# Up projection of a streaming encoder step: the loads of the sample weights are ordered behind the raw weights of the next feature tile

## The chip, the cores and the metric

The kernel runs on one core of one Trainium2 chip. The metric is the device time of one execution in microseconds (us), the median of several runs. One further execution was recorded by the hardware profiler; all durations, starts and waits below are from that recording.

## What is computed

One inference step of a one-layer hybrid encoder, for a prompt of 1024 frames (no history) and a sample of 32 frames (with history), both with 1024 features. A mixer with three kinds of heads comes first, then a convolutional feed-forward block. The change lies in that block:

```python
def conv_ffn(xn, buf, w_up, conv_w, conv_b, w_down):
    up = xn @ w_up                                       # (T, 1024) @ (1024, 5632)
    up, buf = causal_dwconv(up, buf, conv_w, conv_b)     # width 3 along the frames
    gate, val = jnp.split(up, 2, axis=-1)
    return (jax.nn.gelu(gate, approximate=True) * val) @ w_down, buf
...
x = x + rms_norm(h, g_mix_post[l])
h, ffn_buf = conv_ffn(rms_norm(x, g_ffn_pre[l]), states[6][l], ffn_w_up[l], ...)
x = x + rms_norm(h, g_ffn_post[l])
```

Everything is float32. The 5632 columns of `w_up` are 44 tiles of 128 features; tile `f` of the gate half and tile 22+`f` of the value half are worked on together, so there are 22 feature tiles.

## The kernel before

The stages run one behind the other on TensorE: input projection with the mixers beside it, output projection, up projection, down projection. Float32 products are made of three matmuls each (`mm3`): weights' high part by the input's high part (line 88), weights' high by the input's low (line 89), weights' low by the input's high (line 90). So every operand is first split into a high part, by a cast on ScalarE (line 93), and a low part, by a subtraction on VectorE (line 94). The first two matmuls of a weight need its cast alone, the third needs the subtraction too.

**The prompt's up projection** (`up_all`, line 1513) multiplies two by two blocks with a Strassen-like scheme: seven products p1 to p7 instead of eight, each of twelve 128x512 matmuls (four blocks of the inner dimension, three matmuls each), 84 for one feature tile. For feature tile f:

- `up_raw` (line 1278) loads the raw weights: two tiles of 512 KB, `wu{f}r` and `wu{22+f}r`, from `w_up`, on SyncE's queue (line 1282). The pool has two buffers for them, so the loads for tile f+1 wait until VectorE has read the last of tile f's.
- `up_operands` (line 1294) makes the seven weight operands: A12, A11, A22 are the raw blocks, S1 to S4 are sums of them (lines 1306 to 1312, VectorE). Each is split by lines 93 and 94. In the trace they read `A_{f}h` and `S_{f}h`.
- `up_block` (line 1334) issues the products: puy gets A12, pux A11 and then S2 and S3, puw S1 and then S4, puz A22. ScalarE copies some sums out of PSUM (`keep`, line 1347, tiles `c_...`), VectorE adds them into the two tiles `uu` (line 1352).
- `up_finish` (line 1433) convolves the finished `uu` of tile f-1: one activation (line 1440) and two scalar_tensor_tensor (line 1442) for each half, a gelu (line 1444), a product (line 1445), and the store of the result `y` to `h_d` (line 1446, SyncE's queue).

**The sample's up projection** is laid beside it by `up_samples` (line 1448). It is 24 rounds (three column groups, eight blocks of the inner dimension each). A round is a load of sample weights `wus` (line 1457, 1 MB, in the third group 768 KB, SyncE's queue) and three or four small matmuls `us` (line 1474). The loads go into a ring of three buffers; the load for round i+3 is issued in the program after the matmuls of round i and waits for them on the chip. Two or three rounds are visited in each feature tile from f=2 to f=10, between the product S1 or A22 and the product S2, and all later products are ordered behind them by

```python
with tc.issue_after(kept["us"].ins) if "us" in kept else ExitStack():
```

**What sets the order.** The order of the instructions on each engine is made when the kernel is built, by a list scheduler with its own estimate of times. `issue_after(x)` gives it a constraint: what is issued inside isn't placed ahead of `x`. `behind["SP"]` is the latest instruction on SyncE that others are ordered by; `up_raw` sets it to the second raw load (line 1282). The sums of down weights (`sum_weights`, line 1572, DRAM to DRAM, `ws_d`) are already ordered by it. The loads of `wus` had no such constraint. SyncE issues in order: an instruction that waits holds all that are behind it.

Of the kernel before, what the change touches and what calls it, by code (L numbers as in the profile page):

```python
# [78 lines left out]
def body(ctx: ExitStack, tc: tile.TileContext, a: dict):  # L79
    nc = tc.nc  # L80
    act, dve, pool, pe, sp = nc.scalar, nc.vector, nc.gpsimd, nc.tensor, nc.sync
# [157 lines left out]
    cols_of, dcs_of, behind = {}, {}, {}  # L239
    HSET = (2, 0, 4, 5)  # L240
    VGD = (lambda b, h: True, lambda b, h: True, lambda b, h: True)
    pws, wo_raw, ring = ExitStack(), [], []
# [1076 lines left out]
    def behind_products():  # L1319
        with ExitStack() as order:  # L1320
            for x in ends[-3:]:
                order.enter_context(tc.issue_after(x))
            return order.pop_all()
# [124 lines left out]
    def up_samples():  # L1448

        closing = ExitStack()  # L1450
        own = closing.enter_context(tc.tile_pool(name="pss", bufs=1, side="right", reuse_waits="tile"))

        def load(i):
            if i < len(ROUNDS):
                g, k = ROUNDS[i]
                nq = UGROUPS[g][1]
                sp.dma_start(ring[i % 3][:, :nq], a["w_us"][8 * g + k, :, :nq])

        smp_u = own.tile([128, NU, 2 + DEC], F32, name="smp_u")
        sp.dma_start(smp_u[:, :, 0:2], a["fcache"])  # L1460
        ring = [wus[:, 0], wus[:, 1], own.tile([128, 4, 512], F32, name="wus2")]
        smp_x = own.tile([128, 8, DEC], F32, name="smp_x")
        sp.dma_start(smp_x, xn_d[:, :, SEQ:])
        i = 0
        for i in range(3):
            load(i)
        yield
        i = 0
        for g, (c0, nq) in enumerate(UGROUPS):
            ps = psf.tile([128, 512], F32, tag="sx", name=f"us{g}", bufs=1)  # L1470
            for k in range(8):
                with behind_products():
                    for q in range(nq):
                        kept["us"] = pe.matmul(ps[DEC * q:DEC * q + DEC], smp_x[:, k, :], ring[i % 3][:, q, :],
                                               start=k == 0, stop=k == 7)
                load(i + 3)
                i += 1
                if k in VISITS:
                    yield
            m = DEC * nq  # L1480
            us = own.tile([128, NF, DEC], F32, tag="us", name=f"usr{g}", bufs=1).rearrange("p f t -> p (f t)")[:, :512]
            act.copy(us[:m], ps[:m])
            yield
            tp = psb.tile([128, 4, 128], F32, tag="big", name=f"ust{g}", bufs=3)
            for b in range(4):
                pe.transpose(tp[:, b, :m], us[:m, 128 * b:128 * b + 128], ident[:m, :m])
            for b in range(4):
                act.copy(smp_u[:, 4 * c0 + b:4 * (c0 + nq):4, 2:2 + DEC], tp[:, b, :m].rearrange("p (q t) -> p q t", t=DEC))
        pool.tensor_copy(fcq, smp_u[:, :, DEC:DEC + 2])
        yield  # L1490
        smp_y = [p3.tile([128, NF, DEC], F32, tag="xg0", name="smp_v", bufs=1), own.tile([128, NF, DEC], F32, tag="us", name="smp_w", bufs=1)]
        def conv(*args, **kw):
            with tc.issue_after(kept["gated"].ins):
                dve.tensor_tensor(*args, **kw)

        for lo, dst in ((0, smp_h), (NF, smp_y[0])):
            js = slice(lo, lo + NF)
            w = [fconv[:, js, s:s + 1].broadcast_to([128, NF, DEC]) for s in range(4)]
            yield
            conv(dst, smp_u[:, js, 2:2 + DEC], w[2], op=ALU.mult)  # L1500
            yield
            conv(dst, dst, w[3], op=ALU.add)
            for s in range(2):
                yield
                conv(smp_y[1], smp_u[:, js, s:s + DEC], w[s], op=ALU.mult)
                yield
                conv(dst, dst, smp_y[1], op=ALU.add)
        yield
        act.activation(smp_h, smp_h, AF.Gelu_apprx_tanh)
        conv(smp_h, smp_h, smp_y[0], op=ALU.mult)  # L1510
        closing.close()
# [672 lines left out]
```

## Time and profile before

| | us |
|---|---|
| median of 3 runs | 1349.72 |
| the runs | 1347.81, 1349.72, 1349.77 |
| the profiled execution | 1349.57 |
| its span, from the first to the last instruction | 1347.8 |
| output projection of the last tokens ends, up projection begins | at 659 |
| first visit of sample rounds | at 714.6 |
| last sample matmul | at 897.2 |
| last store of `h_d` issued | at 1129.7 |

Times such as "at 714.6" are us from the start of the span. A row of the timeline gives the start, the duration, the engine, the line, the operation with its tiles, the count, and in brackets the idle time of the engine ahead of it with the instruction that ended it. A row of the chain gives the start, the time spent and what; it is the chain of work that ended last, followed back from the end. A row of the windows view gives for a stretch of time the busy time of each engine (the number of instructions), then the granted TensorE clock, the busy share of the DMA engines, and GB/s. TensorE matmuls overlap: a 128x512 one is shown with 0.39 us while the next starts 0.23 us after it.

### The profile page before, as it was taken

Reading aid. Unit: us, or ns where it says so; the run is one execution under the profiler, and the core shown is the slowest. Engines: PE = TensorE matmul, PEld = TensorE weight load, DVE = VectorE, ACT = ScalarE, POOL = GpSimd, SP = SyncE. Lnnn points to the kernel's source line nnn. Section 1 sums busy time; section 2 is a strip of 40 time slices with the busy share of each in tenths; the row PEclk is TensorE's granted clock in tenths of the full one; section 3 lists DMA queues with packets and bytes.
Section 4 is the critical chain, followed back from the end, with each engine's and each line's share of the span. In section 5 each row is a group of like instructions: output and inputs, shape, how many; then the busy total and the mean of one; then the engine's idle time right before and its main releaser. Section 6 shows DMA issues by size and latency. Waiting matters only on the chain.

```text
span 1347.8 us, 25583 instructions
## 1 busy us (share of the span) xinstructions
PE 1302.1 (97%) x9896; PEld 1100.3 (82%) x9896; DVE 1006.8 (75%) x1761; ACT 699.9 (52%) x1298; POOL 281.8 (21%) x400
## 2 busy tenths in 40 slices
PE   6999999999999998999999999999999999999997
PEld 6999889998888987867886767778888887778885
DVE  5795649778698778875797677768888876499566
ACT  5555556554575555534764444445454544454552
POOL 4532303135022254313110010111110000020004
PEclk9999989999998999989999999999999999999999
DMA  9799868886789954543436978865655249844425
GB/s 343 245 354 370 276 230 257 280 281 217 275 246 313 335 190 131 188 134 117 165 106 195 336 212 290 214 191 145 168 153 147 81 137 350 330 161 139 144 88 125
DMA packets 134784, 291.73 MB, mean 216 GB/s; under 512 B 29015, under 2 KB 63991, under 8 KB 132535
## 3 DMA queue, kind: packets, MB, share of 16 engines
q1 hardware_dynamic: 120887, 266.51, 57.8%
q0 software_dynamic: 9264, 19.14, 7.8%
q10 hardware_dynamic: 4512, 4.46, 1.0%
q8 instruction: 77, 1.26, 0.4%
q14 instruction: 44, 0.36, 0.1%
HBM read 229.38 MB, written 85.78 MB: 234 GB/s over the span
## 4 chain that ended last, share of the span: by engine, by line
PE 60%; DVE 8%; ACT 3%; DMA 3%; issue 2%; POOL 1%; SPq 0%; DVEq 0%; POOLq 0%; ACTq 0%
PE pux_None L88 4%; PE pux_None L90 4%; PE pux_None L89 4%; PE q L88 3%; PE q L90 3%; PE q L89 3%; PE puw_None L90 3%; PE puw_None L89 3%; PE puw_None L88 3%; PE x L88 2%; PE x L89 2%; PE x L90 2%; PE zp L90 2%; PE zp L88 2%; PE zp L89 2%
## 5 line engine op out<-in xcount | busy, mean ns | idle before, releaser
L1442 DVE SCALAR_TENSOR_TENSOR y<-uu,fconv_sb,y 128x1024 f32<-128x1024 f32 x88 | 112.7, 1281 | 26.3 <-ACT y L1440 25.4
L1439 POOL COPY fhalo<-uu 128x2 f32<-128x2 f32 x44 | 17.7, 403 | 389.9 <-DVE uu L1352 385.5
L1440 ACT ACTIVATE y<-uu,fconv_sb 128x1024 f32<-128x1024 f32 x44 | 54.7, 1244 | 22.5 <-DVE uu L1352 21.8
L90 PE MATMUL zp<-woh,cl 128*128 128x512 f32 (+1 forms) x144 | 58.2, 404 | 1.5 <-DVE cl L1091 1.5
L88 PE MATMUL zp<-woh,ch 128*128 128x512 f32 (+1 forms) x144 | 57.9, 411 | 1.0 <-ACT ch L1090 0.7
L89 PE MATMUL zp<-wol,ch 128*128 128x512 f32 (+1 forms) x144 | 58.4, 406 | 0.3 <-DVE wol L94 0.3
L88 PE MATMUL pv<-wt_0h,xh 128*128 128x256 f32 (+1 forms) x192 | 55.7, 290 | 3.1 <-DVE xl L319 1.6
L90 PE MATMUL pv<-wt_1h,xl 128*128 128x256 f32 (+1 forms) x192 | 55.1, 287 | 0.0
L88 PE MATMUL pv<-wt_1h,xh 128*128 128x256 f32 (+1 forms) x192 | 54.6, 284 | 0.0
L90 PE MATMUL pv<-wt_0h,xl 128*128 128x256 f32 (+1 forms) x192 | 54.5, 284 | 0.0
L89 PE MATMUL pv<-wt_0l,xh 128*128 128x256 f32 (+1 forms) x192 | 54.3, 283 | 0.0
L89 PE MATMUL pv<-wt_1l,xh 128*128 128x256 f32 (+1 forms) x192 | 54.3, 283 | 0.0
L206 POOL TENSOR_SCALAR hrs<-hss 128x5 f32<-128x5 f32 (+3 forms) x27 | 10.1, 375 | 181.6 <-DVE hss L1000 177.1
L1717 POOL TENSOR_TENSOR gss<-gss 128x1 f32<-128x1 f32 (+1 forms) x9 | 9.9, 1096 | 176.8 <-ACT gjk L1710 176.8
L816 DVE COPY_PREDICATED P<-masks_sb,sc 128x352 f32<-128x352 int32 (+3 forms) x53 | 37.8, 713 | 4.9 <-PE sc L729 4.3
L88 PEld LDWEIGHTS pv<-wt_0h,xh 128*128 128x128 f32 x192 | 35.9, 187 | 4.8 <-DVE xl L319 2.1
L1000 DVE TENSOR_REDUCE hss<-sq 128x5 f32<-128x320 f32 (+3 forms) x27 | 13.5, 502 | 31.5 <-ACT sq L999 31.4
L207 POOL TENSOR_TENSOR hrs<-hrs,mhalf 128x5 f32<-128x5 f32 (+3 forms) x27 | 36.2, 1341 | 2.2
L88 PEld LDWEIGHTS pv<-wt_1h,xh 128*128 128x128 f32 x192 | 36.0, 188 | 0.7 <-issue 0.6
L90 PEld LDWEIGHTS pv<-wt_1h,xl 128*128 128x128 f32 x192 | 36.0, 187 | 0.3
L90 PEld LDWEIGHTS pv<-wt_0h,xl 128*128 128x128 f32 x192 | 36.0, 187 | 0.2
L89 PEld LDWEIGHTS pv<-wt_0l,xh 128*128 128x128 f32 x192 | 36.0, 188 | 0.1
(1899 smaller groups left out, 4645.8 us busy)
## 6 DMA issues: line engine op xcount, KB each, us to landing
wus<-in_w_us SPq DMA_DIRECT2D x16, 1024.0 KB, 6.2
wrP<-in_w_dn SPq DMA_DIRECT2D x27, 512.0 KB, 4.2
ht<-h_d SPq DMA_DIRECT2D x22, 512.0 KB, 7.5
wt_0r<-in_w_tok SPq DMA_DIRECT2D x21, 512.0 KB, 6.0
wt_1r<-in_w_tok SPq DMA_DIRECT2D x21, 512.0 KB, 6.6
h_d<-y SPq DMA_DIRECT2D x21, 512.0 KB, 3.1
ws_d<-in_w_dn POOLq DMA_DIRECT2D x20, 512.0 KB, 6.8
wrP<-ws_d SPq DMA_DIRECT2D x20, 512.0 KB, 3.9
```

The lines of the kernel that those rows point to most:

```text
L88: pe.matmul(ps, lh[0], rh[0], start=first, stop=False, **kw)
L89: pe.matmul(ps, lh[0], rh[1], start=False, stop=False, **kw)
L90: return pe.matmul(ps, lh[1], rh[0], start=False, stop=last, **kw)
L206: pool.tensor_scalar(out, ss, 1.0 / width, eps, op0=ALU.mult, op1=ALU.add)
L207: pool.tensor_tensor(out, out, mhalf[:n, :cols], op=ALU.pow)
L816: dve.copy_predicated(dst, mk.broadcast_to([n, 11, *mk.shape[2:]]), src)
L1000: dve.tensor_reduce(ss[:n, h0:h0 + nh], sq3, axis=mybir.AxisListType.X, op=ALU.add)
L1439: behind["POOL"] = pool.tensor_copy(fhalo[:, j, :], u[:, SEQ - 2:SEQ])
L1440: act.activation(y, u, AF.Identity, scale=fconv[:, j, 2:3], bias=fconv[:, j, 3:4])
L1442: dve.scalar_tensor_tensor(y, uu[i][:, s:s + SEQ], fconv[:, j, s:s + 1], y, op0=ALU.mult, op1=ALU.add)
L1717: pool.tensor_tensor(ss[:n, 0:1], ss[:n, 2:3], ss[:n, 3:4], op=ALU.add)
```

## The change

The load of a `wus` buffer is put under an `issue_after(behind["SP"].ins)`: it is not placed ahead of the raw weights of the next feature tile, as far as these were issued in the program by then.

```diff
@@ -1454,7 +1454,8 @@
             if i < len(ROUNDS):
                 g, k = ROUNDS[i]
                 nq = UGROUPS[g][1]
-                sp.dma_start(ring[i % 3][:, :nq], a["w_us"][8 * g + k, :, :nq])
+                with tc.issue_after(behind["SP"].ins):
+                    sp.dma_start(ring[i % 3][:, :nq], a["w_us"][8 * g + k, :, :nq])
```

No instruction is added or taken away, and no tile changes. The scheduler's order differs on SyncE, TensorE, ScalarE and VectorE between feature tiles 2 and 8, and from there on it is the same as before; on GpSimd it is the same throughout. Line numbers after 1457 are one higher in the changed kernel.

**SyncE, feature tiles 3 and 4.** `wu3r`, `wu25r` are the raw weights of tile 3, `wu4r`, `wu26r` those of tile 4; `y_9235`, `y_9373`, `y_9529` are the results of tiles 0, 1, 2. Before:

```order
L1446 DMA h_d<-y_9235 128x1024
L1457 DMA wus<-in_w_us 128x2048 x2
L1282 DMA wu3r<-in_w_up 128x1024
L1282 DMA wu25r<-in_w_up 128x1024
L1583 DMA ws_d<-in_w_dn 128x2x512 x2
L1446 DMA h_d<-y_9373 128x1024
L1446 DMA h_d<-y_9529 128x1024
L1457 DMA wus_9305<-in_w_us 128x2048
L1457 DMA wus<-in_w_us 128x2048
L1282 DMA wu4r<-in_w_up 128x1024
L1457 DMA wus<-in_w_us 128x2048
L1282 DMA wu26r<-in_w_up 128x1024
```

And now, from the same store on:

```order
L1446 DMA h_d<-y_9235 128x1024
L1282 DMA wu3r<-in_w_up 128x1024
L1282 DMA wu25r<-in_w_up 128x1024
L1584 DMA ws_d<-in_w_dn 128x2x512 x2
L1446 DMA h_d<-y_9373 128x1024
L1458 DMA wus<-in_w_us 128x2048 x2
L1282 DMA wu4r<-in_w_up 128x1024
L1282 DMA wu26r<-in_w_up 128x1024
L1584 DMA ws_d<-in_w_dn 128x2x512 x3
L1446 DMA h_d<-y_9529 128x1024
L1458 DMA wus_9305<-in_w_us 128x2048
L1458 DMA wus<-in_w_us 128x2048 x2
```

The raw loads of tile 3 now stand ahead of two sample loads, and those of tile 4 ahead of the store of tile 2's result and of the three sample loads behind it. Further up, the first three sample loads have moved from ahead of `wu2r`, `wu24r` to right behind them.

**VectorE, feature tile 6.** `A_6h` and `S_6h` are operands made from `wu6r`, `wu28r`; `uu...<-c_5None,...` are the evictions of tile 5, `y_10016` and `y_10021` its convolution. Before:

```order
L94 TENSOR_TENSOR S_5h<-wu27r,S_5h 128x512
L1352 TENSOR_TENSOR uu_8877<-c_5None,puw_None 128x512
L1442 SCALAR_TENSOR_TENSOR y_10016<-uu_8877,fconv_sb,y_10016 128x1024
L1352 TENSOR_TENSOR uu_8878<-c_5None,pux_None 128x512
L1352 TENSOR_TENSOR uu_8878<-c_5None,puz_None 128x512
L1442 SCALAR_TENSOR_TENSOR y_10016<-uu_8877,fconv_sb,y_10016 128x1024
L94 TENSOR_TENSOR A_6h<-wu6r,A_6h 128x512 x2
```

And now, from the second A_6 row on, to the same eviction of puw and what follows it:

```order
L94 TENSOR_TENSOR A_6h<-wu6r,A_6h 128x512
L1442 SCALAR_TENSOR_TENSOR y_9856<-uu_8878,fconv_sb,y_9856 128x1024 x2
L94 TENSOR_TENSOR A_6h<-wu28r,A_6h 128x512
L1445 TENSOR_TENSOR y_9851<-y_9851,y_9856 128x1024
L1306 TENSOR_TENSOR wu28r<-wu28r 128x512
L1309 TENSOR_TENSOR wu28r<-wu6r,wu28r 128x512
L94 TENSOR_TENSOR S_6h<-wu28r,S_6h 128x512
L1310 TENSOR_TENSOR wu6r<-wu28r,wu6r 128x512
L1312 TENSOR_TENSOR wu6r<-wu6r 128x512
L94 TENSOR_TENSOR S_6h<-wu6r,S_6h 128x512
L1352 TENSOR_TENSOR uu_8877<-c_5None,puw_None 128x512
L94 TENSOR_TENSOR S_6h<-wu6r,S_6h 128x512
```

The split of A_6 and most of S_6 now stands ahead of the eviction of tile 5's puw, no longer behind it and the convolution. The casts on ScalarE have moved in the same way, and so has the work for tiles 4, 5 and 7.

**TensorE, start of feature tile 2**, a piece of the difference (`S_1h` is tile 1, `A_2h` tile 2):

```order
 L89 MATMUL puw_None<-B22l,S_1h 128x512
 L90 MATMUL puw_None<-B22h,S_1h 128x512
+L88 MATMUL puy_None<-B21h,A_2h 128x512
+L89 MATMUL puy_None<-B21l,A_2h 128x512
+L88 MATMUL pux_None<-B11h,A_2h 128x512
+L89 MATMUL pux_None<-B11l,A_2h 128x512
 L88 MATMUL pux_None<-T3h,S_1h 128x512
 L89 MATMUL pux_None<-T3l,S_1h 128x512
```

The first four matmuls of tile 2 now stand ahead of the last product of tile 1. For tiles 4, 5 and 6 all twelve A12 matmuls have moved ahead of the twelve S3 matmuls of the tile before; tiles 7 and later had that order already.

## The prediction

> **What bounds the kernel now.** The windows view comes first, for the stretch that the change touches and for all that follows it.
>
> ```profile
> span 1347.8 us, 25583 instructions
> 700.00:812.00 112.00, 107.87 (x517) 78.58 (x516) 80.65 (x105) 50.08 (x77) 9.87 (x15) 1.00 0.73 238
> 812.00:1300.00 488.00, 488.00 (x2215) 388.86 (x2214) 374.01 (x516) 241.43 (x389) 42.50 (x58) 1.00 0.61 186
> ```
>
> The first number behind the stretch's length is TensorE. From 812 to 1300 it is busy all of 488.00 us, so what it loses or gains before 812 moves the end one for one, as long as nothing else takes over. From 700 to 812 it is idle for 112.00 - 107.87 = 4.13 us, and the granted clock is 1.00 in both stretches: the idle time costs no clock besides. VectorE has 80.65 of 112 us, so TensorE is the bound here, with holes in it.
>
> Where the holes are, and what they cost with their restart, is read from TensorE's timeline: the visits of sample matmuls (line 1474) are milestones, one in each feature tile.
>
> ```profile
> 714.61 1.92 PE L1474 MATMUL us<-wus,smp_x 128*32 128x512 f32 x16
> ...
> 725.79 0.50 PE L88 MATMUL puy_None<-B21h,A_3h 128*128 128x512 f32 x1 [0.83 <-ACT A_3h L93]
> ...
> 736.96 2.78 PE L1474 MATMUL us<-wus,smp_x 128*32 128x512 f32 x24
> ...
> 748.67 0.50 PE L88 MATMUL puy_None<-B21h,A_4h 128*128 128x512 f32 x1 [0.52 <-ACT A_4h L93]
> ...
> 759.84 2.78 PE L1474 MATMUL us<-wus,smp_x 128*32 128x512 f32 x24
> ...
> 783.07 1.92 PE L1474 MATMUL us<-wus,smp_x 128*32 128x512 f32 x16
> ...
> 794.61 0.50 PE L88 MATMUL puy_None<-B21h,A_6h 128*128 128x512 f32 x1 [1.19 <-ACT A_6h L93]
> ...
> 797.28 0.50 PE L90 MATMUL puy_None<-B21h,A_6h 128*128 128x512 f32 x1 [1.43 <-DVE A_6h L94]
> ...
> 807.50 2.78 PE L1474 MATMUL us<-wus,smp_x 128*32 128x512 f32 x24
> ...
> 829.49 2.78 PE L1474 MATMUL us<-wus,smp_x 128*32 128x512 f32 x24
> ```
>
> Between the last two lies a tile without a wait: 829.49 - 807.50 = 21.99 us for 84 product matmuls and a visit of 24. A visit of 16 is 2.78 - 1.92 = 0.86 us shorter, so its tile should take 21.13. Against that:
>
> - first interval (tile 3's operands arrive in it): 736.96 - 714.61 = 22.35, **1.22 us** too long;
> - second (tile 4's): 759.84 - 736.96 = 22.88, **0.89 us** too long;
> - third (tile 5's): 783.07 - 759.84 = 23.23. It also holds four transposes of 0.44 us (row below), so 22.43 is due and **0.80 us** too much;
> - fourth (tile 6's): 807.50 - 783.07 = 24.43 against 21.13, **3.30 us** too long.
>
> Together 6.21 us, somewhat over the idle time of 4.13: the intervals also hold what each restart of the stream costs. All these waits are on the first operands of the next tile's weights. Why these are late is read from the chain of waits:
>
> ```profile
> 716.60 0.67 SPq L1457
> 717.37 7.67 DMA wu3r<-in_w_up
> 725.12 0.63 ACT A_3h L93
> ...
> 738.21 1.17 DVE S_3h L94 x2
> 739.38 8.54 DMA wu4r<-in_w_up
> 748.00 0.63 ACT A_4h L93
> ...
> 768.44 0.70 DVE uu L1352
> ...
> 771.64 0.70 DVE A_5h L94
> ...
> 777.67 0.44 PE ust L1486 x4
> ...
> 790.84 0.70 DVE uu L1352
> ...
> 795.43 1.19 DVE y L1442
> 796.62 0.61 DVE A_6h L94
> ```
>
> There are **two causes**. For tiles 3 and 4 it is the raw load itself, 7.67 and 8.54 us from issue to use. For tiles 5 and 6 it is VectorE's order: the split of A_5 and A_6 stands behind the eviction of the last tile's puw (line 1352) and its convolution (1442).
>
> **The change, part by part.** No instruction comes or goes, so the sum is made of waits.
>
> *The loads of tile 3.* SyncE's timeline shows what is ahead of them, and the same load with a free queue is found at tile 7:
>
> ```profile
> 668.64 1.70 SPq L1457 DMA_DIRECT2D wus<-in_w_us  x2
> ...
> 689.33 1.26 SPq L1457 DMA_DIRECT2D wus<-in_w_us  x1
> 693.95 0.33 SPq L1282 DMA_DIRECT2D wu2r<-in_w_up  x1
> 694.55 0.33 SPq L1282 DMA_DIRECT2D wu24r<-in_w_up  x1
> 705.85 0.33 SPq L1446 DMA_DIRECT2D h_d<-y  x1
> 715.74 1.53 SPq L1457 DMA_DIRECT2D wus<-in_w_us  x2
> ...
> 719.74 17.41 SPq L1446 DMA_DIRECT2D h_d<-y  x2
> ...
> L1282 SPq DMA_DIRECT2D wu7r<-in_w_up x1: 334/334/334, 806.9 to 806.9; - x1
> ...
> DMA to landing us min/median/max: 3.5/3.5/3.5
> ...
> wus<-in_w_us SPq DMA_DIRECT2D x16, 1024.0 KB, 6.2
> ```
>
> Two sample loads of 1 MB are issued 1.6 us ahead of `wu3r`; it takes 7.67 us, `wu7r` 3.5. So 2 MB ahead cost 4.2 us, 2.1 us for 1 MB. Now nothing is ahead of `wu3r` but the store at 705.85, long gone. It still waits for its buffer (VectorE's last read, below), so it can't be issued much before 717.
>
> ```profile
> 716.53 0.68 DVE L94 TENSOR_TENSOR S_2h<-wu24r,S_2h 128x512 fp32r<-128x512 f32 x1
> 722.38 0.69 DVE L1352 TENSOR_TENSOR uu<-c_2None,puw_None 128x512 f32<-128x512 f32 x1 [4.03 <-PE puw_None L90]
> ```
>
> It lands near 717 + 3.5 = 720.5; with the cast of 0.63 the high part is there at 721.2, and TensorE needed it at 725.79 - 0.83 = 724.96. The wait goes: **-1.22 us**. The low part fits into the 4.03 us in which VectorE stands idle up to 722.38. The second cast and the eviction that shifts by one subtraction (0.68) have several us of cover.
>
> *The loads of tile 4.* `wu4r` waits for its buffer until `S_3h` is split (738.21, 1.17). That split is now earlier, since tile 3's operands come 4.2 us earlier and are no longer behind the convolution in the order; I bound its gain between 0 and 4.2 us. Issue is then between 735.2 and 739.4. Ahead of it on the queue are two sample loads that go out as soon as tile 1's store has gone, near 720: drained by then. With 3.5 us and the cast it is ready between 739.3 and 743.5. TensorE now wants A_4 earlier: twelve A12 matmuls stand ahead of S3 of tile 3. Tile 3's visit starts at 736.96 - 1.22 = 735.74, takes 2.78, and S2 and S4 take 24 matmuls of (21.99 - 2.78) / 84 = 0.229 us, 5.5 us: 744.0. Ready in time at both bounds, by 0.5 us at the late one: **-0.89 us**. At the late bound the third matmul could wait for a subtraction, 0.7 us at most.
>
> *Tiles 5 and 6.* Their splits now stand ahead of the eviction and convolution of the tile before. What can be late is the load. `wu5r` waits for the S4 split of tile 4, which stands right behind the eviction of tile 3's puw: TensorE ends that product at 744.0, so 744.0 + 0.70 + 0.68 = 745.4; landing 748.9, against a need one tile later, 744.0 + 21.99 = 766.0. Tile 6 is the same with 22.4 us more. **-0.80 and -3.30 us.** If the order of the splits helped not at all, these 4.1 us would stay.
>
> *The three first sample loads* move from 668 to 689 to just behind `wu24r`, near 695. They are needed at 714.61 (two of them). At 2.1 us for 1 MB, 4 MB from 694 on are through at 702.4, at most 3.5 later landed. With 6.2 us each, one behind the other (the median from issue to landing in the row above), two are there at 707.4 and all three at 713.6. Cost 0; the cover is 7 to 12 us, and behind it every us would hold all products, since they are ordered behind the visit.
>
> *Sample loads of later visits* are issued up to some us later, for a visit a whole tile (22 us) on: 0. The eviction of puw and the store of `h_d` now stand behind the next tile's weights on VectorE and SyncE; if a raw load were late, the eviction would be late too. The PSUM tile that it frees is needed two tiles later: 0. The two casts of A_2 moved ahead of a copy out of PSUM on ScalarE delay tile 1's last product by up to 1.1 us, while four matmuls (0.9 us) have moved in ahead of it: 0, at most 0.2.
>
> **Sum:** -1.22 - 0.89 - 0.80 - 3.30 = -6.21 us from the profiled execution's 1349.57 (1347.8 of span and 1.8 around it), which is the median of the runs, 1349.72, but for 0.15. That gives 1343.4.
>
> **Rivals.**
>
> *A, half the gain.* The two loads come in time, but the VectorE terms don't go: something else is as late for A_5 and A_6 (their 4.10 us stay). Only -2.11 us: 1347.5. For it: the waits of tiles 5 and 6 aren't on a DMA now. Against it: tiles 7 and later have this very order of products and splits before the change, and TensorE has no wait in them (488.00 of 488.00).
>
> *B, it is hidden anyway.* The raw loads wait for their buffers as before, land no earlier against the need, and the waits only change their name: 1349.6. Against it: the row of `wu3r` shows the queue, not the buffer, as the longer part (7.67 against 3.5).
>
> *C, slower: more sample loads ahead of the raw loads of tiles 5 and 6.* All three loads of a visit now stand right ahead of `wu5r`, 3 MB instead of 2. If all were issued together, `wu5r` would take 3.5 + 3 x 2.1 = 9.8 us. TensorE has A12 of the next tile ahead of a product that is ready, and stands for all of the lateness; three tiles (4, 5, 6) at, say, 4.5 us each (8.54 us of load instead of 3.5 at tile 4's late bound: 739.4 + 8.5 + 0.6 = 748.5 against 744.0) are 13.5 - 6.2 = +7.3: 1356.9. It decides from 6.2/3 = 2.1 us of lateness per tile on. Against it: the sample loads are gated by the visit's matmuls, near 738, and `wu5r` by the eviction at 745.4, 7 us later, when 6.3 us of queue are gone; and even with 9.8 us it lands at 755.2, 10 us before the need.
>
> The rule behind C is in the Trainium skill, "DMA: Bandwidth & Descriptors", section "Queues, rings and completion order": each DMA engine takes the descriptors of one ring in order, so what is issued first on a queue is served first. By that rule alone C's 9.8 us hold, and the trace agrees with it in the 7.67 us of `wu3r`.
>
> **How the numbers follow.** The forecast, 1343.4: 0.76; by the spread of the three runs (1347.81 to 1349.77) its own range is 1341.6 to 1345.5. A: 0.12. B: 0.05. C: 0.07. A measurement of this kernel can tell about 0.2% (2.7 us) from no change: A and B count as the same, C as slower. Faster 0.76, same 0.17, slower 0.07. The range for 8 in 10 takes in the forecast's with its lower end and half of A: 1341.5 to 1347.5.
>
> **What would show it.** Right: the visits of line 1475 stand 21.1, 22.0, 22.4, 21.1 and 22.0 us apart from the first on; no wait of TensorE on an `A_` operand from 700 to 810; the chain holds no load of `wu3r` or `wu4r`; these land some 3.5 to 4.5 us after issue. Wrong: a wait on `us<-wus` at the first visit (the three first loads), a wait on `A_4h` to `A_6h` ahead of S3 (C), waits on `puw` or `pux` tiles (late evictions), or holes that appear after 812, where there are none now.

## The result, and the profile after

| | before | after |
|---|---|---|
| median | 1349.74 us (6 runs, 1347.81 to 1352.12) | 1340.60 us (6 runs, 1335.34 to 1343.22) |
| ratio | | 0.9942, 95% interval 0.9919 to 0.9965 |
| the profiled execution | 1349.57 us, span 1347.8 | 1338.15 us, span 1336.4 |
| first product of the up projection begins | at 659.25 | at 653.98 |
| from there to the end of the span | 688.5 | 682.4 |

By the medians the changed kernel is faster by 9.1 us; the ratio comes to 7.8 us, with an interval of 4.7 to 10.9 us. First TensorE's timeline of the changed kernel, the visits of sample matmuls, one in each feature tile from tile 2 on, as before:

```profile
709.36 1.92 PE L1475 MATMUL us<-wus,smp_x 128*32 128x512 f32 x16
...
730.52 2.78 PE L1475 MATMUL us<-wus,smp_x 128*32 128x512 f32 x24
...
752.51 2.78 PE L1475 MATMUL us<-wus,smp_x 128*32 128x512 f32 x24
...
774.95 1.92 PE L1475 MATMUL us<-wus,smp_x 128*32 128x512 f32 x16
...
796.08 2.78 PE L1475 MATMUL us<-wus,smp_x 128*32 128x512 f32 x24
...
818.07 2.78 PE L1475 MATMUL us<-wus,smp_x 128*32 128x512 f32 x24
```

They stand 21.16, 21.99, 22.44, 21.13 and 21.99 us apart, where they stood 22.35, 22.88, 23.23, 24.43 and 21.99 us apart before. From the first to the last it is 108.71 us, before 114.88: 6.17 us less. The windows view agrees (columns as before: length, then busy time of TensorE, its weight loads, VectorE, ScalarE, GpSimd, then clock, DMA share, GB/s):

```profile
690.00:830.00 140.00, 140.00 (x679) 105.87 (x677) 107.44 (x139) 69.30 (x103) 14.14 (x20) 1.00 0.84 279
830.00:1300.00 470.00, 470.00 (x2124) 375.64 (x2123) 358.44 (x498) 234.32 (x386) 42.11 (x60) 1.00 0.57 176
```

TensorE's first column equals the length in both: no idle time is left. The view of TensorE's waits has no row at all from 690 to 1000. What became of the loads is on SyncE's timeline of the changed kernel; the number behind the start is the time of the issue, not of the transfer:

```profile
711.39 0.33 SPq L1282 DMA_DIRECT2D wu3r<-in_w_up  x1
712.00 0.33 SPq L1282 DMA_DIRECT2D wu25r<-in_w_up  x1
712.37 1.29 SPq L1584 DMA_DIRECT2D ws_d<-in_w_dn  x2
713.76 0.56 SPq L1446 DMA_DIRECT2D h_d<-y  x1
714.41 1.19 SPq L1458 DMA_DIRECT2D wus<-in_w_us  x2
728.09 0.33 SPq L1282 DMA_DIRECT2D wu4r<-in_w_up  x1
729.89 0.33 SPq L1282 DMA_DIRECT2D wu26r<-in_w_up  x1
730.26 1.88 SPq L1584 DMA_DIRECT2D ws_d<-in_w_dn  x3
732.25 0.57 SPq L1446 DMA_DIRECT2D h_d<-y  x1
732.93 1.89 SPq L1458 DMA_DIRECT2D wus<-in_w_us  x3
741.28 0.33 SPq L1282 DMA_DIRECT2D wu5r<-in_w_up  x1
```

`wu3r` is now 3.0 us ahead of its two sample loads. The tile views of `wu3r` and `wu5r` give the landing, and ScalarE's timeline, with the wait of the cast in brackets, that of `wu4r` (issued at 728.09):

```profile
L1282 SPq DMA_DIRECT2D wu3r<-in_w_up x1: 328/328/328, 711.4 to 711.4; - x1
DMA to landing us min/median/max: 3.6/3.6/3.6
...
L1282 SPq DMA_DIRECT2D wu5r<-in_w_up x1: 327/327/327, 741.3 to 741.3; - x1
DMA to landing us min/median/max: 9.1/9.1/9.1
...
732.04 1.14 ACT L93 CAST A_4h<-wu4r 128x512 fp32r<-128x512 f32 x2 [2.63 <-DMA wu4r<-in_w_up]
...
750.37 0.62 ACT L93 CAST A_5h<-wu5r 128x512 fp32r<-128x512 f32 x1 [2.19 <-DMA wu5r<-in_w_up]
...
760.82 0.39 PE L88 MATMUL puy_None<-B21h,A_5h 128*128 128x512 f32 x1
```

`wu3r` takes 3.6 us (before 7.67) and `wu4r` 3.9 (before 8.54). But `wu5r` takes 9.1 us, and its cast waits 2.19 us for it. That costs nothing: TensorE asks for A_5 only at 760.82 (last row, TensorE's timeline), 10.4 us after the cast began.

### The profile page after: what moved, and what is told of

Read it like the earlier page. It is cut to its first block, busy times and chain, and to the rows that moved or that the text cites. A ratio compares the mean times of both kernels' runs of the same rounds, so it can differ in the third digit from the quotient of the medians.

```text
span 1336.4 us, 25589 instructions
## 1 busy us (share of the span) xinstructions
PE 1295.7 (97%) x9896; PEld 1097.9 (82%) x9896; DVE 1009.2 (76%) x1761; ACT 700.0 (52%) x1298; POOL 284.6 (21%) x400
## 4 chain that ended last, share of the span: by engine, by line
PE 63%; DVE 9%; ACT 2%; issue 1%; POOL 1%; DMA 0%; DVEq 0%; POOLq 0%; ACTq 0%
PE pux_None L88 4%; PE pux_None L90 4%; PE pux_None L89 4%; PE puw_None L89 3%; PE puw_None L90 3%; PE puw_None L88 3%; PE q L88 3%; PE q L89 3%; PE q L90 3%; PE x L88 2%; PE x L89 2%; PE x L90 2%; PE zp L88 2%; PE zp L90 2%; PE zp L89 2%; PE us L1475 2%
## 5 line engine op out<-in xcount | busy, mean ns | idle before, releaser
L1440 ACT ACTIVATE y<-uu,fconv_sb 128x1024 f32<-128x1024 f32 x44 | 54.7, 1244 | 12.8 <-DVE uu L1352 12.2
L90 PE MATMUL zp<-woh,cl 128*128 128x512 f32 (+1 forms) x144 | 57.0, 396 | 1.5 <-DVE cl L1091 1.5
L90 PE MATMUL pv<-wt_1h,xl 128*128 128x256 f32 (+1 forms) x192 | 55.1, 287 | 0.0
L90 PE MATMUL pv<-wt_0h,xl 128*128 128x256 f32 (+1 forms) x192 | 54.8, 286 | 0.0
L90 PEld LDWEIGHTS pv<-wt_0h,xl 128*128 128x128 f32 x192 | 36.4, 189 | 0.2
L89 PEld LDWEIGHTS pv<-wt_1l,xh 128*128 128x128 f32 x192 | 36.2, 189 | 0.1
```

What stands on the lines that cost most here:

```text
L89: pe.matmul(ps, lh[0], rh[1], start=False, stop=False, **kw)
L90: return pe.matmul(ps, lh[1], rh[0], start=False, stop=last, **kw)
L1440: act.activation(y, u, AF.Identity, scale=fconv[:, j, 2:3], bias=fconv[:, j, 3:4])
```

## The experiments

The kernels e2, e3, e4 and e9 differ from the changed one in a single line, which says which of the 24 sample loads are under the constraint. The table gives, for each kernel, the four intervals that had waits, then the time from the first product of the up projection to the end of the span (which leaves out all that comes ahead of the changed stage), and the device time (the median where there are several runs).

| kernel | tile 3 | tile 4 | tile 5 | tile 6 | first product to end | time |
|---|---|---|---|---|---|---|
| before | 22.35 | 22.88 | 23.23 | 24.43 | 688.5 | 1349.74 |
| after | 21.16 | 21.99 | 22.44 | 21.13 | 682.4 | 1340.60 |
| e1, before again | 22.86 | 22.80 | 23.24 | 24.40 | 689.0 | 1349.46 |
| e2, rounds 3 and 4 alone | 21.16 | 22.00 | 22.43 | 21.13 | 682.4 | 1342.06 |
| e3, rounds 0 to 2 alone | 22.77 | 22.75 | 23.29 | 24.39 | 688.8 | 1346.70 |
| e4, rounds 5 to 23 | 23.17 | 21.99 | 22.43 | 21.13 | 684.4 | 1346.53 |
| e5, late splits | 21.16 | 22.00 | 22.49 | 21.13 | 682.4 | 1340.71 |
| e6, early splits | 22.46 | 22.80 | 25.93 | 21.44 | 688.3 | 1351.12 |
| e7, ScalarE's queue | 21.92 | 27.65 | 22.43 | 21.13 | 688.9 | 1349.65 |
| e8, no sample loads | 21.16 | 22.00 | 22.43 | 21.13 | 682.6 | 1338.39 |
| e9, round 3 alone | 21.16 | 23.20 | 23.23 | 27.27 | 690.5 | 1347.44 |
| e10, loads twice | 21.16 | 27.30 | 33.11 | 21.13 | 704.5 | 1366.35 |
| e11, after again | 21.16 | 21.99 | 22.43 | 21.13 | 682.4 | 1340.90 |
| e12, early split of tile 6 alone | 22.68 | 22.75 | 23.23 | 23.51 | 687.9 | 1347.62 |

A device time of one run is worth little here: runs of the kernel before went from 1340.57 to 1353.40 us. Where nothing is late the intervals repeat within 0.1 us and the column beside them within 0.2, and the verdicts rest on them.

**e1, the kernel before once more**, with no edit.

> The kernel before, profiled once more. In the first two profiles the first up-projection matmul (puy of tile 0) stands at 659.25 us before and at 653.98 us after the change, although nothing ahead of it differs. Theory 'drift': that is a difference between executions, by the granted clock of the stages ahead, so this second profile may put it anywhere from 650 to 662, while the intervals between the visits of sample matmuls repeat within 0.1 us: 22.35, 22.88, 23.23, 24.43, 21.99. Rival 'real': the changed kernel truly starts the up projection 5 us earlier; then this one stands at 659 +- 1 again.

All four intervals came back, tile 3's with 0.5 us more (its wait was 1.36 us here, 0.83 the first time). So the first term of the prediction, -1.22 us, is one draw from 1.2 to 1.7 (2.0 in e4). The first product began at 658.71, where the rival had it; the theory of drift allows that too, so this run alone decides nothing, and all fourteen profiles are compared further down.

**e2, the constraint on the two sample loads of rounds 3 and 4 alone**, those that stood ahead of `wu3r`:

```diff
-                with tc.issue_after(behind["SP"].ins):
+                with tc.issue_after(behind["SP"].ins) if i in (3, 4) else ExitStack():
```

> The order is imposed on two of the 24 sample loads alone, those of rounds 3 and 4, which stood right ahead of the raw loads of tile 3. Theory 'one start': once wu3r is early, the scheduler's order for tiles 4 to 8 follows by itself; all four terms go, intervals 21.1, 22.0, 22.4, 21.1, about 6.2 us faster than before. Theory 'each its own' (the prediction's two causes, each tile with its own queue): tile 3 loses its 1.22 us, and the other terms (0.89, 0.80, 3.30) stay at least by half: intervals 21.1, 22.4 to 22.9, 22.8 to 23.2, 22.8 to 24.4, 1.2 to 3.7 us faster.

Two loads of 24 bring the whole gain: 1342.06 us (5 runs) against 1347.87 of the kernel before beside it (8 runs), ratio 0.995, interval 0.9929 to 0.997. No TensorE wait is left, though `wu4r` to `wu6r` have no constraint ahead of them. The order that the scheduler made shows why: behind tile 2, the rows of SyncE, VectorE and ScalarE are those of the changed kernel, one for one. I take it that once tile 3's weights come early in its estimate, it places the raw loads of the later tiles ahead of the sample loads by itself; the order shows the outcome, and the estimate stands in no trace.

**e3, the constraint on rounds 0 to 2 alone** (`if i < 3`):

> The order is imposed on the first three sample loads alone. Both theories: no gain from these; intervals as before (22.35, 22.88, 23.23, 24.43 within 0.2), first visit 55.4 us behind the first up-projection matmul as in both kernels. Rival 'first loads': if the move of the first three loads had shortened the stretch up to the first visit, it would be under 54 us here.

No gain, as the prediction had it for this part: the intervals are those of before, and from the first product to the first visit it is 55.34 us, before 55.36. One wait has another name. Before, tile 5's only wait was 0.16 us on VectorE's subtraction; here, with the same interval, it is on the cast, and the cast waited for the load. ScalarE's and TensorE's timelines:

```profile
767.86 1.14 ACT L93 CAST A_5h<-wu5r 128x512 fp32r<-128x512 f32 x2 [0.36 <-DMA wu5r<-in_w_up]
...
768.53 0.50 PE L88 MATMUL puy_None<-B21h,A_5h 128*128 128x512 f32 x1 [0.42 <-ACT A_5h L93]
```

`wu5r` was issued at 759.33 in this kernel, so it took 8.5 us behind two sample loads, and was itself what tile 5 waited for.

**e4, all but rounds 0 to 4** (`if i > 4`). Its one wait is in TensorE's timeline:

> The order is imposed on the loads of rounds 5 to 23 alone: the two loads ahead of wu3r stay where they were, those ahead of wu4r, wu26r and of later raw loads go behind. Prediction's terms: tile 3 keeps its 1.22 us (22.35), the load of wu4r takes 3.5 to 4.5 us in place of 8.5 and tiles 4 to 6 lose their terms: intervals 22.35, 22.0, 22.4, 21.1; 5.0 us faster. Theory 'one start': with tile 3 late, tile 4 is late too, since its buffer is released late, and part of the rest stays: second interval 22.4 or more.

```profile
727.71 0.50 PE L88 MATMUL puy_None<-B21h,A_3h 128*128 128x512 f32 x1 [1.62 <-ACT A_3h L93]
```

Tile 3 keeps its wait of 1.62 us and an interval 2.0 us too long, and tiles 4 to 6 are free. So the terms of tile 3 and of the later tiles can be had apart; the later ones don't need tile 3 to be early.

**e9, the constraint on round 3 alone** (`if i == 3`), which leaves 1 MB ahead of `wu3r` in place of 2:

> The order is imposed on the load of round 3 alone: one sample load, not two, stands ahead of wu3r, and from the store of tile 1's result on the order is that of the kernel before. By 2.1 us for 1 MB wu3r takes about 5.7 us in place of 7.7, lands 2 us earlier, and tile 3's wait of 1.0 to 1.7 us goes (first interval 21.1 to 21.4). Theory 'separable': tiles 4 to 6 keep their waits, since their queue and order are as before: 22.8, 23.2, 24.4. Rival 'one start': tile 4's buffer is free earlier because tile 3 was earlier, and at least half of the 5 us goes as well.

The tile view of `wu3r` in this kernel:

```profile
L1282 SPq DMA_DIRECT2D wu3r<-in_w_up x1: 378/378/378, 712.6 to 712.6; - x1
DMA to landing us min/median/max: 5.8/5.8/5.8
```

3.6 us with nothing ahead, 5.8 with 1 MB, 7.67 with 2 MB: the price of 2.1 us for 1 MB holds for these three (what it leaves out is taken up in the next section). In e3 and e4 the same `wu3r` took 8.1 and 8.4 us behind 2 MB, up to 2.4 us for 1 MB. Tile 3's wait goes (4.2 us of lead aren't needed, 2 are enough), those of tiles 4, 5 and 6 stay. So it takes both loads to turn the scheduler's order over. The long fourth interval is a matter of the clock and is read in the last section.

**e8, no sample loads from round 3 on**, in the kernel before (the sample's matmuls run on what the three buffers hold, so its result is left out):

```diff
-            if i < len(ROUNDS):
+            if i < 3:
```

> The kernel before without the sample loads of rounds 3 to 23 (the matmuls use what the three buffers hold). It is the ceiling of what moving these loads can bring. Theory: the changed kernel is there already, TensorE has no wait in tiles 3 to 8, so the intervals are the same 21.1, 22.0, 22.4, 21.1, 22.0 within 0.1. Rival: loads still slow something (the DMA engines, 24 issues on SyncE), and without them the intervals are shorter by over 0.2 us.

Its intervals are those of the changed kernel, to 0.01 us, and so is the time from the first product on (682.6 against 682.4). The change has all that moving the sample loads can give.

**e5, the change with late splits**: the operands of tiles 5 and 6 are made behind the eviction of the last tile's puw, as they were before the change, with the loads early.

```diff
+            kept[f"out{i}{j}"] = dve.tensor_tensor(uu[i][:, c:c + n], x, ps, op=op)
...
-                if s != 0 and f + 1 < NF:
+                if s != 0 and f + 1 < NF and f not in (4, 5):
...
+                if f in (4, 5):
+                    with tc.issue_after(kept["out01"].ins):
+                        ops = up_operands(f + 1, raw.pop(f + 1))
+                        W[f + 1] = next(ops)
+                        for _ in ops:
+                            pass
```

> The changed kernel, with the splits of the weights of tiles 5 and 6 put behind the eviction of puw of the tile before (their place relative to it before the change); the loads stay early. Prediction's theory (order on VectorE makes the waits of tiles 5 and 6): some of 0.80 and 3.30 us comes back, third and fourth interval together 44.6 us or more (43.57 in the changed kernel). Rival 'the loads made it': with the loads early the split right behind the eviction is still in time (eviction one matmul stream of 2.7 us ahead of the need), intervals 22.4 and 21.1 within 0.3, and what cost time before was the convolution that the scheduler had put in between.

VectorE's, ScalarE's and TensorE's timelines of this kernel around A_6:

```profile
784.94 0.69 DVE L1352 TENSOR_TENSOR uu<-c_5None,puw_None 128x512 f32<-128x512 f32 x1 [6.49 <-PE puw_None L90]
785.54 1.29 DVE L94 TENSOR_TENSOR A_6h<-wu6r,A_6h 128x512 fp32r<-128x512 f32 x2
...
780.50 1.14 ACT L93 CAST A_6h<-wu6r 128x512 fp32r<-128x512 f32 x2 [2.56 <-DMA wu6r<-in_w_up]
...
784.64 0.39 PE L88 MATMUL puy_None<-B21h,A_6h 128*128 128x512 f32 x1
...
788.72 0.39 PE L90 MATMUL puy_None<-B21h,A_6h 128*128 128x512 f32 x1
```

The subtraction (L94) stands behind the eviction (L1352) again, and nothing waits. Two things cover it: the casts are done 3 us ahead of the first matmul, and the scheduler, knowing the split to be late, has put the first matmul that needs the low part (L90) 4.1 us behind that first one, with products of the high part between. Before the change there were three matmuls and a wait between them. So "behind the eviction" is no cause by itself. The convolution, which before the change stood ahead of the split as well, stands behind it here, so this run does not test the convolution's place.

**e6, the kernel before with early splits**: no constraint on the loads, and the eviction of puw of tiles 4 and 5 held back behind the split of the next tile's A blocks. SyncE's order changed with it, as expected: the raw loads of tile 6 went out ahead of the sample loads (`wu6r` landed 3.3 us after its issue), those of tile 5 still behind two of them.

```diff
-        (eng or pool).tensor_tensor(lo, src, hi.bitcast(F32), op=ALU.subtract)
+        kept["low"] = (eng or pool).tensor_tensor(lo, src, hi.bitcast(F32), op=ALU.subtract)
...
+            kept[f"split{f}"] = kept["low"]
...
-        out(0, 1, c6, w)
+        with tc.issue_after(kept[f"split{f + 1}"].ins) if f in (4, 5) else ExitStack():
+            out(0, 1, c6, w)
```

> The kernel before, with its sample loads as they were up to tile 5, and the evictions of puw of tiles 4 and 5 put behind the split of A22 of tiles 5 and 6. SyncE's order changes with it: wu6r, wu28r now stand ahead of the sample loads, wu5r still behind two of them. Both theories: 22.4 to 22.9 and 22.8 for tiles 3 and 4 as before. Tile 6: its wait goes (21.1 to 21.4), by its free load and by the order. Tile 5 tells them apart: if VectorE's order made its wait, it goes (22.4); if the late load made it, the load takes 7 to 9 us again and the interval is 23.2 or longer.

TensorE's timeline of this kernel, and the window around it:

```profile
781.48 0.50 PE L88 MATMUL puw_None<-T1h,S_5h 128*128 128x512 f32 x1 [0.24 <-ACT S_5h L93]
...
783.57 0.50 PE L90 MATMUL puw_None<-T1h,S_5h 128*128 128x512 f32 x1 [1.35 <-DVE S_5h L94]
...
780.00:790.00 10.00, 8.42 (x36) 4.42 (x35) 9.44 (x11) 5.95 (x13) 0.00 (x0) 0.83 0.62 134
```

Tile 6's wait went, by its early load or by the new order, which this run doesn't tell apart. Tile 5 got a new one, on S_5, whose operands now stood behind what had been held back. The two intervals come to 47.37 us, before 47.66, with no waits 43.56. Some 1.7 us of it is the clock (0.83 in these 10 us); without that, this kernel would have had about half of the 4.1 us. Moving an order that the scheduler chose moved the lateness.

**e12, the same for tile 6 alone** (`if f == 5`), which leaves tile 5 and all of SyncE's order as before:

> The kernel before, with VectorE's order changed at one place alone: the eviction of puw of feature tile 5 (and the convolution that follows it) stands behind the split of A_6. SyncE's order stays: wu6r is still issued behind two sample loads of 1 MB. It separates the two causes of tile 6's wait, which cost 3.30 us in the fourth interval between visits (24.43 against 21.13). Theory 1, order alone (the prediction's term): the fourth interval is 21.1 to 21.5, no wait on A_6h. Theory 2, both: in the kernel before the high part came 1.19 us late (its cast began at 793.94, with the load behind 2 MB on the queue) and the low part another 1.43 us late, behind the convolution; without the latter some 1.43 us and a part of the restart go, and the interval is 22.3 to 23.0, with a wait of 0.5 to 1.5 us on ACT A_6h and none on DVE A_6h. Theory 3, load alone: the low part waits for the load too, the interval stays at 24.1 to 24.7. The first three intervals stay as before (22.3 to 22.9, 22.8 to 22.9, 23.2 to 23.3). If the granted clock falls behind the wait, as it did in another run of the same waits (0.80 in the 17 us behind it, 2.9 us), the interval is up to 2.9 longer, and the granted clock of that stretch shows it. Time under theory 2: about 1.6 us less than the kernel before, not to be told from one run; the intervals decide.

ScalarE's, VectorE's and TensorE's timelines of this kernel:

```profile
792.41 0.59 ACT L1348 COPY c_5None<-pux_None 128x512 f32<-128x512 f32 x1 [4.80 <-PE pux_None L90]
792.89 1.14 ACT L93 CAST A_6h<-wu6r 128x512 fp32r<-128x512 f32 x2
...
794.30 1.28 DVE L94 TENSOR_TENSOR A_6h<-wu6r,A_6h 128x512 fp32r<-128x512 f32 x2
...
793.57 0.50 PE L88 MATMUL puy_None<-B21h,A_6h 128*128 128x512 f32 x1 [1.19 <-ACT A_6h L93]
...
795.04 0.50 PE L90 MATMUL puy_None<-B21h,A_6h 128*128 128x512 f32 x1 [0.22 <-DVE A_6h L94]
```

The wait for the low part fell from 1.43 to 0.22 us, the interval from 24.43 to 23.51, which lies between the second and the third theory. So VectorE's order held 0.92 us of tile 6's 3.30. The wait for the high part, 1.19 us, stayed to the digit. In the rows it is ScalarE's order: the cast stands behind the copy of pux, the copy waits for TensorE's last matmul on pux, and TensorE then wants the cast. In the changed kernel the first cast of A_6h (767.80) is placed ahead of that copy (769.18). But the load may have been as late as the copy. To cover the need, a cast had to start by 791.8 (TensorE stood from 792.38, and a cast takes 0.6). `wu6r` was issued at 784.43 behind two sample loads, and loads in that place took 7.67 us (`wu3r` before) to 8.5 (`wu5r` in e3): by this estimate it landed between 792.1 and 792.9, too late for the need wherever the cast stood. Its landing is not on record, so the load's share and ScalarE's aren't told apart.

**e7, the kernel before with the sample loads on ScalarE's queue** (`act.dma_start` in place of `sp.dma_start`, no constraint). Do the raw loads suffer from the order in one queue, or from the DMA engines that all queues share?

> The kernel before, with all sample loads issued from ScalarE's queue, so that nothing is ahead of the raw loads on SyncE's, while the two sample loads ahead of tile 3 still go out at the same time (716). Theory 'queue order': wu3r no longer stands behind 2 MB; it shares the DMA engines with them and takes 4 to 6 us in place of 7.7 to 8.5; tile 3's wait falls from 1.2 to 2.0 us to under 0.5. Rival 'bandwidth': the DMA engines are what is full, and it takes 7 us or more on another queue as well; the wait stays. Other tiles aren't told apart by this run; ScalarE also pays for 24 issues.

The page's row on the sample loads of this kernel, then ScalarE's and TensorE's timelines:

```profile
wus<-in_w_us ACTq DMA_DIRECT2D x16, 1024.0 KB, 8.0
...
725.08 0.62 ACT L93 CAST A_3h<-wu25r 128x512 fp32r<-128x512 f32 x1 [0.69 <-DMA wu25r<-in_w_up]
...
748.29 1.24 ACT L1440 ACTIVATE y<-uu,fconv_sb 128x1024 f32<-128x1024 f32 x1 [1.42 <-DVE uu L1352]
749.44 1.12 ACT L93 CAST A_4h<-wu4r 128x512 fp32r<-128x512 f32 x2
...
750.09 0.80 PE L88 MATMUL puy_None<-B21h,A_4h 128*128 128x512 f32 x1 [3.85 <-ACT A_4h L93]
```

Both, so neither theory as it stood. Tile 3's wait went but for 0.16 us, so the order in the queue mattered. But the second raw load, `wu25r`, issued at 715.77 with no sample load ahead of it on its queue, was there only at 725.08, 9.3 us later (4.2 in the changed kernel), and the sample loads took 8.0 us instead of 6.2: the queues share the engines. Tile 4's wait, 3.85 us, is the worst single one of all these kernels but for e10's, and in the rows no load ended it: the cast stood behind the convolution's activation (L1440) on ScalarE. How much of it the order made alone isn't shown: `wu4r` was issued at 738.00, its landing is not on record, and if it took the 9.3 us of `wu25r` (an estimate) it was there at 747.3, when TensorE had already stood for 1.1 us.

**e10, the change with each sample load from round 3 on made twice**, to double what the raw loads stand beside:

```diff
                 with tc.issue_after(behind["SP"].ins):
                     sp.dma_start(ring[i % 3][:, :nq], a["w_us"][8 * g + k, :, :nq])
+                    if i > 2:
+                        sp.dma_start(ring[i % 3][:, :nq], a["w_us"][8 * g + k, :, :nq])
```

> The changed kernel with every sample load from round 3 on made twice into the same buffer (the second waits for the first on SyncE's queue). It asks how much cover the raw loads of tiles 4 to 6 have, since wu5r takes 9.1 us in the changed kernel and not the 3.5 of the prediction. Twice the data and some 6 to 8 us of waiting on SyncE for each pair. Rival C (more data ahead of the raw loads makes TensorE stand) from 2.1 us of lateness on. My theory: the need lies 13 us or more behind the landing of wu5r, so tiles 5 and 6 lose 0 to 4 us together; tile 4 (wu4r lands some 5 us ahead of its need) 0 to 3; all in all 0 to 6 us slower than the changed kernel. If it is under 0.3 the cover is larger than the queue of two visits; if it is over 10 the prediction's C was far nearer than its 0.07.

TensorE's waits from 690 to 850 in this kernel are one row:

```profile
PE us L1477 <- DMA wus<-in_w_us: 12.9, 5, 6.1
```

I had looked for the raw loads to become late, by 0 to 6 us in all, and missed: it is 25.5 us slower than e11 beside it, 22.1 us of that from the first product on, and not by them. `wu4r` took 9.3 us and TensorE never waited for it. The sample loads themselves were late, five times, up to 6.1 us. So the order of the change has its price on that side: what now stands at the queue's end is what the visits need, and its cover is less than a second helping of the loads takes.

**e11, the changed kernel once more**, in 12 runs.

> The changed kernel once more, five rounds against the kernel before. Theory 'drift': the ratio comes nearer to the 6.2 us of the four terms than in the first measurement (0.9942): 0.9954, between 0.994 and 0.997; intervals 21.16, 21.99, 22.44, 21.13 again, and the first up-projection matmul anywhere from 653 to 661. Rival 'real': a further 2 to 5 us come from ahead of the up projection: ratio 0.994 or less, first matmul at 654 +- 1.

1340.90 us against 1347.52 of the kernel before (17 runs): ratio 0.9956, interval 0.9938 to 0.9974; by the medians 6.6 us less. The intervals and the 682.4 us from the first product on are those of the first profile.

## Why the prediction was right, and where not

**The sum, -6.21 us: right.** By the visits it is 6.17, by the time from the first product to the end 6.1 (688.5 to 682.4), by the longer comparison 6.6 (5.9 by its ratio). All five intervals came as foretold, 21.1, 22.0, 22.4, 21.1 and 22.0. The first comparison showed 9.1 us by the medians, and its profile 11.4. The forecast of the time came out less well than that of the gain: the median, 1340.60, is 2.8 us below 1343.4, and 0.9 below the lower end of the stated range, 1341.5. The ratio, 0.9942 of the 1349.72 that the prediction started from, gives 1341.9. Of the profile's 11.4, 5.3 us stand ahead of the changed stage: the up projection began at 653.98 in place of 659.25, with the same instructions in the same order ahead of it. Windows of before and, behind the dots, of after:

```profile
600.00:653.00 53.00, 50.38 (x359) 41.12 (x358) 27.42 (x47) 23.64 (x50) 12.14 (x22) 0.96 0.45 146
...
600.00:653.00 53.00, 50.38 (x368) 41.38 (x367) 31.47 (x50) 26.35 (x54) 12.13 (x22) 1.00 0.42 139
```

The granted clock there was 0.96 and 1.00. Taken over all windows of 10 us up to 650, the time that the clock withheld (the window's length times one less its granted clock, added up) was 15.3 us before and 10.3 after, 5.0 us apart where the starts are 5.3 apart. Over all fourteen profiles the up projection began between 653.96 and 660.76, and later where more was withheld (10.2 to 17.1 us, correlation 0.80). In the five kernels whose sample loads kept their places up to tile 5 or left the queue (before, e1, e6, e12, e7) the mean start was 658.9, in the nine others 656.5; the mean time withheld was 14.7 and 12.5. I put this down to drift of the granted clock in the stages ahead; that the change has a share in it, by a way that no row shows, is left open.

**Tiles 3 and 4, -1.22 and -0.89: right, by their own cause.** The queue was it: 3.6 and 5.8 us with none and one sample load ahead (after, e9), and the wait of tile 3 is there exactly as long as both are (e1, e3, e4 against e2, e9). One bound of the working was too narrow: relative to the first visit `wu4r` was issued 6.0 us earlier, and I had allowed 4.2. It did no harm, being on the good side.

**Tiles 5 and 6, -0.80 and -3.30: right in size, wrong in cause.** "For tiles 5 and 6 it is VectorE's order" is the step that failed. With the loads early, the split right behind the eviction costs nothing (e5). With the loads late, moving the eviction and the convolution behind the split by hand gives 0.92 of tile 6's 3.30 us (e12). What the runs show in its place is late loads: tile 5's own load is what ended its wait in e3, at an unchanged interval of 23.29, and the waits of tiles 5 and 6 are gone in every kernel whose raw loads for them were early by the order on the queue, late tile 3 or not (after, e2, e4, e5, e7, e8). In all of these but e5 VectorE's order had moved as well, so for tile 6 e5 and e12 carry the argument. How much of the rest of tile 6's wait is the load and how much ScalarE's order, a cast behind a copy that I had not read, stays open. That both sizes were right is in part luck: each term was the whole gap to a tile without waits, and such a term comes out whatever made the wait, if only the change removes it. I take all of these orders for one thing, the list scheduler's answer to loads that it took to be late, since two early loads turn the whole of it over (e2). Rival A, that these terms stay, was the right place to doubt, and fell because with the loads early nothing was late for A_5 and A_6, with the splits ahead of the eviction (after) or behind it (e5).

**The queue ahead of `wu5r`: wrong.** "6.3 us of queue are gone" by the time it is issued, and 3.5 us to land: it took 9.1, near to rival C's 9.8. I had counted only the three sample loads; in the 3 us ahead of them, three copies of down weights and a store had gone out on the same queue. The rate was too fast as well: 2.1 us for 1 MB is what the raw load lost after the sample loads' head start, 1.6 us for two and 0.4 for one. Counted from the first issue on, `wu3r` landed after 3.6, 6.2 and 9.3 us with none, one and two sample loads ahead (after, e9, before), so 1 MB held it up for 2.6 to 3.1 us, and 3 MB are some 8 to 9 us of queue, not 6.3 (an estimate). The windows of the changed kernel and, behind the dots, of e8 show both parts:

```profile
733.00:741.00 8.00, 8.00 (x38) 6.43 (x35) 6.68 (x11) 3.45 (x7) 0.27 (x1) 1.00 0.99 354
...
733.00:741.00 8.00, 8.00 (x38) 6.49 (x35) 6.45 (x11) 3.42 (x6) 0.42 (x1) 1.00 0.84 281
```

Up to 741 the DMA engines (next to last number) were full at 0.99, and at 0.84 even without sample loads. In e8 `wu5r` was cast at most 4.8 us after its issue, so the sample loads make at least 4.3 of the 9.1. The rule of the Trainium skill that the prediction cites ("DMA: Bandwidth & Descriptors", "Queues, rings and completion order"), that each DMA engine takes the descriptors of one ring in order, fits these 4.3 us. They do not prove it, since `wu25r` of e7 took 9.3 us with no sample load ahead of it on its queue. What kept rival C from coming true was only its other half, the cover: 10 us at tile 5, as the prediction had it.

**The three first sample loads, 0: right** (e3; 55.38 us from the first product to the first visit, before 55.36).

## What to carry to other kernels

Read a hole in the bounding engine from the load that is late, and then ask what the scheduler made of that lateness on every other engine: waits a tile or two later, on another engine's order, may be the same fault. Then try the smallest constraint that brings the first load early; here two loads of 24 did all. And before a load is put behind others, count everything on the queue, copies and stores too, and set its landing against the need: 9 us in a full queue cost nothing here, since there were 10 us of cover.

## What was not expected of the hardware

**The clock falls behind short waits, in some runs.** In e9 the waits of tile 6 were those of before, 1.19 and 1.42 us, but the interval was 27.27 us in place of 24.43. TensorE's timeline of e9, and the windows of e9 and, behind the dots, of before:

```profile
792.02 0.80 PE L90 MATMUL puy_None<-B21h,A_6h 128*128 128x512 f32 x1 [1.42 <-DVE A_6h L94]
792.61 0.63 PE L88 MATMUL puy_None<-B21h,A_6h 128*128 128x512 f32 x1
793.03 0.63 PE L89 MATMUL puy_None<-B21l,A_6h 128*128 128x512 f32 x1
...
789.00:798.00 9.00, 7.23 (x18) 5.38 (x19) 9.00 (x12) 4.14 (x6) 1.32 (x2) 0.63 0.65 145
...
793.00:802.00 9.00, 6.38 (x27) 4.49 (x26) 8.98 (x11) 4.82 (x7) 1.32 (x2) 1.00 0.80 207
```

For 5.7 us the matmuls start 0.43 us apart in place of 0.23, half the rate, which costs 2.8 us beside the wait. The same waits left the clock at 1.00 in before, e1 and e3. It fell also behind the 1.59 us in e6 and the 3.85 in e7. The Trainium skill ("TensorE: Matmul & The Clock Gate", "Part 1: The HAM clock gate (the "warmup" mystery)") has the clock halve after an idle window of about 3.4 us; here it halved once behind 1.59 us, in two pieces within 2.5 us, and behind 2.61 us in one of four kernels, so the measured idle can be well under the page's. What sets it off in one run and not in another isn't shown. A wait that is taken away may thus be worth more than it reads: in e9 2.61 us of waits cost 6.14 us of interval, before 3.30.

**A queue of its own is no bandwidth of its own**: e7's 9.3 us for a load of 512 KB with no sample load ahead of it on its queue, against 4.2.
